# A decoder block with three token mixers: rotation halves copied by DMA, inputs loaded a step ahead, other orders of work

## The chip, the cores and the metric

One core of a Trainium2 chip runs the whole program. The metric is the device time of an execution in microseconds. A core has TensorE (PE: matmuls and transposes into PSUM), VectorE (DVE), ScalarE (ACT), GpSimd (POOL), and SyncE (SP), which here only issues DMAs. Each of them works through its own list of instructions in order and waits on semaphores.

## The reference

The input is x, 1024 rows of 1024 float32 values, with the weights of one layer:

```
h = RMSNorm(x);  P = h @ W_in                      # 1024 x 9248, split by columns
a = retention(rotary(rq), rotary(rk), rv)          # 4 heads of 128, chunks of 128
    rotary(x1|x2) = (x1*cos - x2*sin | x1*sin + x2*cos)
a = (silu(rg) * group_norm(a)) @ ret_w_o
b = group_norm(ssd(conv(sxbc), dt) * silu(sz)) @ ssd_w_o     # 16 heads of 64, 2 groups
c = (silu(gr) * group_norm(gla(gq, gk, gv, gate))) @ gla_w_o # 4 heads, keys 64, values 128
x = x + (sig(g_a)*a + sig(g_b)*b + sig(g_c)*c) @ W_out
x = x + relu(RMSNorm(x) @ W_up)^2 @ W_down
y = RMSNorm(x)
```

Retention, SSD and GLA are recurrences over eight chunks of 128 rows: a product inside the chunk, and a state carried on to the next.

## The kernel before

All arithmetic is at float32 accuracy, made from three matmuls in the faster format `fp32r`: every operand is split into a rounded part and its remainder (`split`, lines 155 to 157: ScalarE rounds, VectorE subtracts), and `acc3` (line 159) adds high x high, high x low and low x high in PSUM. Nearly all of TensorE's matmuls stand at line 164, and most weights pass through `wslot` (line 150): a DMA into one of two raw buffers, then a split into one of four pairs.

*Start.* `x_rows` (line 227) loads 128 rows and scales them by their norm, `x_chunk` transposes them on TensorE (line 244) and splits the result (`he` for even chunks, `ob` and `hb` for odd ones); `v_unit` (line 284) multiplies a chunk by the value weights.

*Projections.* `run_set` (line 340) computes 256 columns of P by seven products instead of eight (Strassen's scheme): seven steps of 12 matmuls each, with partial sums `us` on VectorE (line 358) that the next product into the same PSUM bank must wait for. `projections` (line 387) goes through the sets, prepares the next set's weights in between, and after each step runs one function of the list `later`. For four of the sets (rotary q and k of two head pairs) a result tile goes through `e_rot` (line 420): `turn` multiplies each half of 64 partitions by sin into the other half of `rb` (line 433), multiplies the tile by cos (line 434), adds both on GpSimd (line 435) and stores the tile to HBM (line 403).

*Mixers.* `merge` (line 915) interleaves generators: after each step of the main one as many steps of the mixer as its share says. `ret_mixer` (line 596) loads per chunk one tile `rin` of six blocks (q, k and gate of two heads, line 606) into one of three buffers, and `rv` into one of two. `stage_a` makes scores, `stage_b` outputs and the state, and `finish_heads` (line 575) normalizes, transposes (line 589) and multiplies by the gate, which is read from `rin`, one step later. `ssd_mixer` (line 670) runs beside 27 gate steps, and then `ssd_rows` (line 774) takes a power on GpSimd (line 177), transposes and stores it. `gla_mixer` (line 783) loads one tile `gin` of 14 blocks per chunk (line 800) and runs beside the first two branches of the output.

*Output.* For each half of the rows `branch_part` (line 1039) multiplies the heads of one branch (0 retention, 1 SSD, 2 GLA) by its weights, eight steps of 12 matmuls (24 for SSD), multiplies by the gate on VectorE (line 1054) and adds the branches on GpSimd (line 1058). In the last branch the sum is split into `mh` and `ml`, which `out_half` (line 1065) multiplies by W_out, 256 columns at a time; its first 63 matmuls use all but the last of the eight tiles. Normalization and the MLP follow.

The order of instructions on each engine is fixed when the program is built. A planner goes through time by its own estimates of durations and lets an engine take the first instruction, in the order of the program text, whose inputs and buffers are ready. A load can thus stand far ahead of its place in the text, as soon as its buffer is free; its place in the text decides only which of several ready ones goes first. At run time that order doesn't change.

Of the kernel before, what the change touches and what calls it, by code (L numbers as in the profile page):

```python
# [18 lines left out]
P = 128  # L19
# [32 lines left out]
def _layout(inp):  # L52
# [38 lines left out]
    a["c_cos"] = np.ascontiguousarray(np.concatenate([cos, cos]))  # L91
    a["c_sin"] = np.ascontiguousarray(np.concatenate([sin, -sin]))
    lg = np.log1p(-np.exp2(f(-5.0) - np.arange(RH, dtype=f))).astype(f)
# [18 lines left out]
def block_kernel(ctx, tc, i, out):  # L112
# [113 lines left out]

    def x_rows(c):
        xr = pro.tile([P, D], F32, name="xr")
        nc.sync.dma_start(out=xr, in_=i["x"][c])
        sq = pro.tile([P, D], F32, name="xsq", bufs=1)  # L230
        ss = wk.tile([P, 1], F32, name="ssx", tag="ss", bufs=6)
        S.activation(out=sq, in_=xr, func=AF.Square, accum_out=ss)
        v = wk.tile([P, 1], F32, name="vsx", tag="ss", bufs=6)
        V.tensor_scalar(out=v, in0=ss, scalar1=1.0 / D, scalar2=EPS, op0=ALU.mult, op1=ALU.add)
        r = wk.tile([P, 1], F32, name="rsx", tag="ss", bufs=6)
        G.tensor_tensor(out=r, in0=v, in1=nhalf[:, 0:1], op=ALU.pow)
        S.activation(out=xr, in_=xr, func=AF.Copy, scale=r)
        return xr
# [167 lines left out]
    def halves(t):  # L406
        return t.rearrange("p (j q t) -> q p j t", q=2, t=P)
# [12 lines left out]
    def e_rot(p, slot0):  # L420
        def emit(n, par, ps, other):
            r = ev.tile([P, 512], F32, name="ra", tag="w2k")
            if other is None:
                S.copy(out=r, in_=ps)
            else:
                V.tensor_tensor(out=r, in0=ps, in1=other, op=ALU.add)

            def turn():
                b = rp.tile([P, 512], F32, name="rb", tag="rb", bufs=2)
                r3, b3 = (t.rearrange("p (j t) -> p j t", t=P) for t in (r, b))  # L430
                for q in range(2):
                    src, to = slice(64 * q, 64 * q + 64), slice(64 - 64 * q, 128 - 64 * q)
                    V.tensor_tensor(out=b3[to], in0=r3[src], in1=halves(sin)[par][src], op=ALU.mult)
                V.tensor_tensor(out=r3, in0=r3, in1=halves(cos)[par], op=ALU.mult)
                G.tensor_tensor(out=r, in0=r, in1=b, op=ALU.add)
                put_T(rt_d[p], slot0 + n, par, r)
            later.append(turn)
        return emit
# [157 lines left out]
    def ret_mixer(p):  # L596
# [4 lines left out]
        for t, n, w in ((dm, "c_dm", 2 * P), (qd, "c_qd", 2 * P), (kd, "c_kd", 2)):  # L601
            nc.sync.dma_start(out=t, in_=i[n][:, p * w:(p + 1) * w])

        def stage_a(c):
            rin = rm.tile([P, 6, P], F32, name="rin", bufs=3)
            nc.sync.dma_start(out=rin, in_=rt_d[p][c])
            rv = rm.tile([P, 256], F32, name="rv")
            nc.sync.dma_start(out=rv, in_=rv_d[p][c])
            sc = pmx.tile([P, 512], F32, name="mx", tag="mx")
# [19 lines left out]
        def stage_b(c):  # L629
            rin, rv, sm, qs, ks = live.pop(c)  # L630
            state = st["s"]
            o = pmx.tile([P, 512], F32, name="mx", tag="mx")
# [5 lines left out]
            if c + 1 < NT:  # L638
# [12 lines left out]
                st["s"] = new  # L651
            return finish_heads(o[:, 0:256], rin[:, 4:6, :], o_d[p][c // 4][:, :, c % 4, :])

        pend = None
        stage_a(0)
        yield
# [117 lines left out]
    def ssd_rows():  # L774
        r = rstd(wk, ssq, SH // SG * SP, 2 * NT)
        pt = ptp.tile([P, 512], F32, name="tp", tag="tp")
        PE.transpose(out=pt[0:2 * NT, 0:P], in_=r, identity=ident)
        rt = wk.tile([2 * NT, P], F32, name="ysr", tag="whalf", bufs=2)
        V.tensor_copy(out=rt, in_=pt[0:2 * NT, 0:P])
        nc.sync.dma_start(out=ys_d, in_=rt)  # L780


    def gla_mixer():
# [11 lines left out]
        ins = {}  # L795

        def stage_a(c, q_):
            if q_ == 0:
                gin = gp.tile([P, 14, P], F32, name="gin", bufs=3)
                nc.sync.dma_start(out=gin, in_=gt_d[c])  # L800
                ins[c] = gin
            gin = ins[c]
# [129 lines left out]
    for _ in range(24):  # L932
        PE.matmul(out=wz[:, 0:128], lhsT=ones, rhs=ones, start=True, stop=True)
    xn = {0: x_rows(0)}
    w0 = [wslot(i["w_vdg"][q], 1152) for q in range(2)]
    xn[1] = x_rows(1)
    w1 = [wslot(i["w_v"][q]) for q in range(2)]
    hc = {0: x_chunk(0, xn[0])}
    xn[2] = x_rows(2)
    raws, cur = {}, {}  # L940
    for c in range(NT):
        if c + 1 < NT:
            hc[c + 1] = x_chunk(c + 1, xn.pop(c + 1))
            if c + 3 < NT:
                xn[c + 3] = x_rows(c + 3)
            if c % 2 == 0:
                x_comb(c // 2)
        v_unit(c, hc[c], 0, w0)
        if c < NT - 2:
            v_unit(c, hc[c], 1, w1)  # L950
        if c == 3:
            raws[0], raws[1] = fetch(jobs[0][1]), fetch(jobs[1][1])
# [34 lines left out]
    rm = rmst.enter_context(tc.tile_pool(name="rm", bufs=2))  # L987
    merge(run(4), 28, itertools.chain(ret_mixer(0), ret_mixer(1)), 38)
    rmst.close()
# [10 lines left out]
    sp = sst.enter_context(tc.tile_pool(name="sp", bufs=2))  # L1000
    merge(itertools.islice(main, 27), 27, itertools.chain(ssd_mixer(0), ssd_mixer(1)), 38)
    ssd_rows()
    sst.close()
# [32 lines left out]

    accs = {}

    def branch_part(h, b, o):
        first = (0, 4, 12)[b]  # L1040
        ws = None
        for d in range(KD):
            if b == 1 or d % 2 == 0:
                ws = wslot(i["w_o"][first + (d if b == 1 else d // 2)])
            pool, tag = (ev, "w2k") if b else (bp, "macc")
            gt = pool.tile([P, 512], F32, name="gt", tag=tag, bufs=8 if b == 0 else 4)
# [8 lines left out]
            if b == 0:  # L1055
                accs[d] = gt
            else:
                G.tensor_tensor(out=accs[d], in0=gt, in1=accs[d], op=ALU.add)
            if b == 2:
                m = (mp.tile([P, 512], F32R, name="mh"), mp.tile([P, 512], F32R, name="ml"))  # L1060
                split(m[0], m[1], accs[d])
                merged[d] = m
            yield

    def out_half(h):
# [4 lines left out]
        for s in range(4):  # L1070
            ws = [wslot(i["w_out"][s, q]) for q in range(2)]
            ps = [None] * 4
# [50 lines left out]
    mixer = gla_mixer()  # L1123
    merge(branch_part(0, 0, o), 8, zip_steps(itertools.islice(parts, 6), itertools.islice(mixer, 6)), 6)
    merge(branch_part(0, 1, o), 8, mixer, 12)
    for _ in parts:
# [6 lines left out]
    mp = mst.enter_context(tc.tile_pool(name="mp", bufs=8, side="right"))  # L1133
    for _ in branch_part(0, 2, o):
        pass
# [6 lines left out]
    merge(rest, 8, load_o(1, o, range(16)), 16)  # L1142
    for b in range(3):
        for _ in branch_part(1, b, o):
            pass
# [177 lines left out]
```

## Time and profile before

| | |
|---|---|
| Time, median of 3 runs | 1921.67 us (1919.79 to 1925.02) |
| Profiled execution, its own time | 1922.45 us |
| Its span | 1920.7 us |
| PE busy | 1870.8 us (97%) |
| DVE busy | 1134.4 us (59%) |
| ACT busy | 825.2 us (43%) |
| POOL busy | 216.3 us (11%) |
| Mean granted clock of PE | 0.993 |

The span runs from the first to the last instruction of the profiled execution. Busy times are shares of the whole span; TensorE's matmuls are pipelined and their ends modelled, so busy doesn't mean at its peak. A row `A <- B` in the list of waits says that A stood still until B was done. In the rows, `L164` is line 164 of the kernel, `SPq` a DMA issued by SP, and a tile's buffer number is left out.

### The profile page before, as it was taken

How to read it: one execution, taken by the hardware profiler on the slowest of the kernel's cores; microseconds unless marked ns; L12 is line 12 of the kernel's file. 1: busy time of each engine (PE TensorE's matmuls, PEld its weight loads, DVE VectorE, ACT ScalarE, POOL GpSimd, SP SyncE). 2: the span in 40 equal slices, each digit the busy share in tenths (PEclk: the TensorE clock that was granted, in tenths of full speed). 3: DMA queues.
4: the chain of work that ended last, by engine and by line, in shares of the span. 5: the costliest groups of instructions: out<-in, count | busy, mean ns of one | idle time of the engine just before them, and what ended most of it. 6: DMA issues, size and time to landing. Idle time of an engine off the chain costs nothing. (4 is left out here: it accounts for less than half of the span.)

```text
span 1920.7 us, 24987 instructions
## 1 busy us (share of the span) xinstructions
PE 1870.8 (97%) x9372; PEld 1542.8 (80%) x9372; DVE 1134.4 (59%) x1719; ACT 825.2 (43%) x1438; POOL 216.3 (11%) x223
## 2 busy tenths in 40 slices
PE   8999999999999999999999999999999999999998
PEld 8977778888777777777888988988888888888886
DVE  6877766667545476746776445585555444444444
ACT  7522333334445597855663113354444431211213
POOL 0011100000121043321232023000000000000003
PEclk9999999999999999999999999999999999999999
DMA  6423323333653666538467543642232362332222
GB/s 215 144 88 98 114 88 119 110 107 92 196 152 116 224 203 192 174 101 284 148 206 257 187 127 121 222 164 103 101 119 93 120 246 89 97 101 88 89 73 92
DMA packets 169465, 271.69 MB, mean 141 GB/s; under 512 B 11616, under 2 KB 110976, under 8 KB 162688
## 3 DMA queue, kind: packets, MB, share of 16 engines
q1 hardware_dynamic: 168768, 269.18, 43.3%
q8 instruction: 74, 1.21, 0.2%
q10 hardware_dynamic: 576, 0.92, 0.1%
q14 instruction: 47, 0.39, 0.1%
HBM read 191.33 MB, written 78.72 MB: 141 GB/s over the span
## 5 line engine op out<-in xcount | busy, mean ns | idle before, releaser
L156 ACT CAST whi<-raw 128x1024 fp32r<-128x1024 f32 (+1 forms) x223 | 233.6, 1050 | 515.4 <-PE mm L164 464.1
L157 DVE TENSOR_TENSOR wlo<-raw,whi 128x1024 fp32r<-128x1024 f32 (+1 forms) x223 | 281.1, 1261 | 127.0 <-ACT whi L156 125.6
L164 PE MATMUL mm<-ht,whi 128*128 128x512 f32 x936 | 296.8, 398 | 6.8 <-DVE us L358 6.8
L164 PEld LDWEIGHTS mm<-ht,whi 128*128 128x128 f32 x936 | 175.5, 188 | 52.1 <-DVE us L358 8.6
L164 PE MATMUL mm<-he,whi 128*128 128x512 f32 x672 | 214.7, 399 | 1.2 <-ACT us L364 0.9
L164 PE MATMUL mm<-whi,ah 128*128 128x512 f32 x512 | 202.5, 395 | 0.0
L164 PE MATMUL mm<-wlo,ah 128*128 128x512 f32 x512 | 202.5, 395 | 0.0
L164 PE MATMUL mm<-whi,al 128*128 128x512 f32 x512 | 202.5, 395 | 0.0
L164 PE MATMUL mm<-ht,wlo 128*128 128x512 f32 x468 | 185.6, 397 | 0.0
L1267 DVE TENSOR_TENSOR x<-mm,x 128x512 f32<-128x512 f32 x128 | 88.2, 689 | 158.8 <-PE mm L164 158.8
L164 PEld LDWEIGHTS mm<-he,whi 128*128 128x128 f32 x672 | 125.2, 188 | 32.4 <-issue 1.7
L164 PE MATMUL mm<-hb,whi 128*128 128x512 f32 x464 | 149.0, 401 | 0.7 <-DMA hb<-b 0.7
L164 PE MATMUL mm<-he,wlo 128*128 128x512 f32 x336 | 133.7, 398 | 0.0
L164 PE MATMUL mm<-ht,w 128*128 128x512 f32 x468 | 116.3, 396 | 0.0
L164 PEld LDWEIGHTS mm<-wlo,ah 128*128 128x128 f32 x512 | 96.2, 188 | 23.4
L164 PEld LDWEIGHTS mm<-whi,ah 128*128 128x128 f32 x512 | 96.2, 188 | 23.2
L164 PEld LDWEIGHTS mm<-whi,al 128*128 128x128 f32 x512 | 96.2, 188 | 23.2
L358 DVE TENSOR_TENSOR us<-mm,us 128x512 f32<-128x512 f32 x78 | 53.8, 690 | 89.1 <-PE mm L164 87.7
L164 PEld LDWEIGHTS mm<-ht,wlo 128*128 128x128 f32 x468 | 88.1, 188 | 21.5
L164 PEld LDWEIGHTS mm<-ht,w 128*128 128x128 f32 x468 | 87.7, 188 | 21.0
L164 PEld LDWEIGHTS mm<-hb,whi 128*128 128x128 f32 x464 | 86.2, 188 | 22.2 <-issue 1.7
L164 PE MATMUL mm<-ohi,whi 128*128 128x512 f32 x256 | 103.9, 406 | 0.0
(281 smaller groups left out, 3544.3 us busy)
## 6 DMA issues: line engine op xcount, KB each, us to landing
raw<-w_in SPq DMA_DIRECT2D x34, 1024.0 KB, 5.4
raw<-w_o SPq DMA_DIRECT2D x32, 512.0 KB, 4.1
raw<-w_up SPq DMA_DIRECT2D x16, 1024.0 KB, 4.9
act<-rl SPq DMA_DIRECT2D x64, 256.0 KB, 2.0
raw<-w_down SPq DMA_DIRECT2D x32, 512.0 KB, 4.3
araw<-act SPq DMA_DIRECT2D x64, 256.0 KB, 3.4
gate<-gt SPq DMA_DIRECT2D x48, 256.0 KB, 2.9
gt<-gate SPq DMA_DIRECT2D x48, 256.0 KB, 4.8
```

The source lines that it names most:

```text
L156: S.copy(out=dst_hi, in_=src)
L157: V.tensor_tensor(out=dst_lo, in0=src, in1=dst_hi.bitcast(F32), op=ALU.subtract)
L164: PE.matmul(out=ps, lhsT=l, rhs=r, start=(first and j == 0), stop=(last and j == n - 1), skip_group_check=open_)
L358: V.tensor_tensor(out=t, in0=ps, in1=other, op=ALU.add)
L1267: V.tensor_tensor(out=xs, in0=ps, in1=xs, op=ALU.add)
```

## The change

Seven edits in one:

- Rotation: two DMAs copy the halves of a result tile crosswise into a tile `rb` as soon as it is made, and `turn` multiplies the tile by cos into a new tile and the copy by sin in place, both over 128 partitions, with the sign now in the constant.
- Retention: q and k blocks and values are loaded by `load_in`, called for chunk c + 1 in `stage_a(c)`; the gate blocks have a tile `rg` of their own, loaded in `stage_b`.
- Start: x rows and first weights are loaded by DMAs that stand first in the text; the first value product stands ahead of the second chunk's work.
- SSD: the mixer runs beside 26 steps, and `ssd_rows` is a generator around the 27th.
- GLA: the first `gin` is loaded, and its memory cleared, ahead of the first branch; the mixer's first step comes after four branch steps instead of two.
- Output: in the last branch the sums of tiles 6 and 7 are on VectorE, and the first W_out weights are fetched at tile 6.
- Second half: branches run in the order 0, 2, 1, so that SSD (24 matmuls per step) is last.

```diff
     a["c_cos"] = np.ascontiguousarray(np.concatenate([cos, cos]))
-    a["c_sin"] = np.ascontiguousarray(np.concatenate([sin, -sin]))
+    a["c_sin"] = np.ascontiguousarray(np.concatenate([-sin, sin]))
     lg = np.log1p(-np.exp2(f(-5.0) - np.arange(RH, dtype=f))).astype(f)
...
-    def x_rows(c):
+    def x_load(c):
         xr = pro.tile([P, D], F32, name="xr")
         nc.sync.dma_start(out=xr, in_=i["x"][c])
+        return xr
...
+    def x_rows(xr):
         sq = pro.tile([P, D], F32, name="xsq", bufs=1)
...
+            b = rp.tile([P, 512], F32, name="rb", tag="rb", bufs=3)
+            for q in range(2):
+                nc.sync.dma_start(out=b[64 - 64 * q:128 - 64 * q], in_=r[64 * q:64 * q + 64])
...
             def turn():
-                b = rp.tile([P, 512], F32, name="rb", tag="rb", bufs=2)
                 r3, b3 = (t.rearrange("p (j t) -> p j t", t=P) for t in (r, b))
-                for q in range(2):
-                    src, to = slice(64 * q, 64 * q + 64), slice(64 - 64 * q, 128 - 64 * q)
-                    V.tensor_tensor(out=b3[to], in0=r3[src], in1=halves(sin)[par][src], op=ALU.mult)
-                V.tensor_tensor(out=r3, in0=r3, in1=halves(cos)[par], op=ALU.mult)
-                G.tensor_tensor(out=r, in0=r, in1=b, op=ALU.add)
-                put_T(rt_d[p], slot0 + n, par, r)
+                a = rp.tile([P, 512], F32, name="rc", tag="rc", bufs=2)
+                a3 = a.rearrange("p (j t) -> p j t", t=P)
+                V.tensor_tensor(out=a3, in0=r3, in1=halves(cos)[par], op=ALU.mult)
+                V.tensor_tensor(out=b3, in0=b3, in1=halves(sin)[par], op=ALU.mult)
+                G.tensor_tensor(out=a, in0=a, in1=b, op=ALU.add)
+                put_T(rt_d[p], slot0 + n, par, a)
             later.append(turn)
...
+        ins = {}
...
+        def load_in(c):
+            rin = rm.tile([P, 4, P], F32, name="rin", bufs=3)
+            nc.sync.dma_start(out=rin, in_=rt_d[p][c][:, 0:4])
+            rv = rm.tile([P, 256], F32, name="rv", bufs=3)
+            nc.sync.dma_start(out=rv, in_=rv_d[p][c])
+            ins[c] = rin, rv
...
         def stage_a(c):
-            rin = rm.tile([P, 6, P], F32, name="rin", bufs=3)
-            nc.sync.dma_start(out=rin, in_=rt_d[p][c])
-            rv = rm.tile([P, 256], F32, name="rv")
-            nc.sync.dma_start(out=rv, in_=rv_d[p][c])
+            if c + 1 < NT:
+                load_in(c + 1)
+            rin, rv = ins.pop(c)
             sc = pmx.tile([P, 512], F32, name="mx", tag="mx")
...
             rin, rv, sm, qs, ks = live.pop(c)
+            rg = rm.tile([P, 2, P], F32, name="rg")
+            nc.sync.dma_start(out=rg, in_=rt_d[p][c][:, 4:6])
             state = st["s"]
...
                 st["s"] = new
-            return finish_heads(o[:, 0:256], rin[:, 4:6, :], o_d[p][c // 4][:, :, c % 4, :])
+            return finish_heads(o[:, 0:256], rg, o_d[p][c // 4][:, :, c % 4, :])
...
         pend = None
+        load_in(0)
+        yield
         stage_a(0)
...
         r = rstd(wk, ssq, SH // SG * SP, 2 * NT)
+        yield
         pt = ptp.tile([P, 512], F32, name="tp", tag="tp")
...
         nc.sync.dma_start(out=ys_d, in_=rt)
+        yield
...
+        def load_in(c):
+            ins[c] = gp.tile([P, 14, P], F32, name="gin", bufs=3)
+            nc.sync.dma_start(out=ins[c], in_=gt_d[c])
...
+        load_in(0)
+        yield
...
         def stage_a(c, q_):
-            if q_ == 0:
-                gin = gp.tile([P, 14, P], F32, name="gin", bufs=3)
-                nc.sync.dma_start(out=gin, in_=gt_d[c])
-                ins[c] = gin
+            if q_ == 0 and c + 1 < NT:
+                load_in(c + 1)
             gin = ins[c]
...
         PE.matmul(out=wz[:, 0:128], lhsT=ones, rhs=ones, start=True, stop=True)
-    xn = {0: x_rows(0)}
-    w0 = [wslot(i["w_vdg"][q], 1152) for q in range(2)]
-    xn[1] = x_rows(1)
+    def v_raw(name, q, n):
+        raw = wp.tile([P, n], F32, name="raw", tag="raw", bufs=2)
+        nc.sync.dma_start(out=raw, in_=i[name][q])
+        return raw
...
+    rows_in = {0: x_load(0)}
+    raw0 = [v_raw("w_vdg", q, 1152) for q in range(2)]
+    rows_in[1] = x_load(1)
+    xn = {0: x_rows(rows_in.pop(0))}
+    w0 = [wparts(None, raw, 1152) for raw in raw0]
+    hc = {0: x_chunk(0, xn.pop(0))}
+    xn[1] = x_rows(rows_in.pop(1))
     w1 = [wslot(i["w_v"][q]) for q in range(2)]
-    hc = {0: x_chunk(0, xn[0])}
-    xn[2] = x_rows(2)
+    rows_in[2] = x_load(2)
     raws, cur = {}, {}
     for c in range(NT):
+        if c == 0:
+            v_unit(c, hc[c], 0, w0)
         if c + 1 < NT:
             hc[c + 1] = x_chunk(c + 1, xn.pop(c + 1))
+            if c + 2 < NT:
+                xn[c + 2] = x_rows(rows_in.pop(c + 2))
             if c + 3 < NT:
-                xn[c + 3] = x_rows(c + 3)
+                rows_in[c + 3] = x_load(c + 3)
             if c % 2 == 0:
                 x_comb(c // 2)
-        v_unit(c, hc[c], 0, w0)
+        if c > 0:
+            v_unit(c, hc[c], 0, w0)
         if c < NT - 2:
...
     rm = rmst.enter_context(tc.tile_pool(name="rm", bufs=2))
-    merge(run(4), 28, itertools.chain(ret_mixer(0), ret_mixer(1)), 38)
+    merge(run(4), 28, itertools.chain(ret_mixer(0), ret_mixer(1)), 40)
     rmst.close()
...
     sp = sst.enter_context(tc.tile_pool(name="sp", bufs=2))
-    merge(itertools.islice(main, 27), 27, itertools.chain(ssd_mixer(0), ssd_mixer(1)), 38)
-    ssd_rows()
+    merge(itertools.islice(main, 26), 26, itertools.chain(ssd_mixer(0), ssd_mixer(1)), 38)
+    tail = ssd_rows()
+    next(tail)
+    merge(itertools.islice(main, 1), 1, tail, 1)
     sst.close()
...
-    def branch_part(h, b, o):
+    first_out = []
...
+    def branch_part(h, b, o, last=False):
         first = (0, 4, 12)[b]
...
                 ws = wslot(i["w_o"][first + (d if b == 1 else d // 2)])
+            if last and d == 6:
+                first_out.extend(wslot(i["w_out"][0, q]) for q in range(2))
             pool, tag = (ev, "w2k") if b else (bp, "macc")
...
             else:
-                G.tensor_tensor(out=accs[d], in0=gt, in1=accs[d], op=ALU.add)
-            if b == 2:
+                (V if last and d > 5 else G).tensor_tensor(out=accs[d], in0=gt, in1=accs[d], op=ALU.add)
+            if last:
                 m = (mp.tile([P, 512], F32R, name="mh"), mp.tile([P, 512], F32R, name="ml"))
...
         for s in range(4):
-            ws = [wslot(i["w_out"][s, q]) for q in range(2)]
+            ws = [first_out.pop(0) if s == 0 else wslot(i["w_out"][s, q]) for q in range(2)]
             ps = [None] * 4
...
     mixer = gla_mixer()
-    merge(branch_part(0, 0, o), 8, zip_steps(itertools.islice(parts, 6), itertools.islice(mixer, 6)), 6)
-    merge(branch_part(0, 1, o), 8, mixer, 12)
+    next(mixer)
+    main = branch_part(0, 0, o)
+    merge(itertools.islice(main, 2), 2, itertools.islice(parts, 2), 2)
+    merge(main, 6, zip_steps(itertools.islice(parts, 4), itertools.islice(mixer, 5)), 5)
+    merge(branch_part(0, 1, o), 8, mixer, 13)
     for _ in parts:
...
     mp = mst.enter_context(tc.tile_pool(name="mp", bufs=8, side="right"))
-    for _ in branch_part(0, 2, o):
+    for _ in branch_part(0, 2, o, True):
         pass
...
     merge(rest, 8, load_o(1, o, range(16)), 16)
-    for b in range(3):
-        for _ in branch_part(1, b, o):
+    for b in (0, 2, 1):
+        for _ in branch_part(1, b, o, b == 1):
             pass
```

## Rows read from the trace of the kernel before

**Rows 1.** The page's busy line of TensorE: us, share of the span, instructions.

```profile
PE 1870.8 (97%) x9372; PEld 1542.8 (80%) x9372; DVE 1134.4 (59%) x1719; ACT 825.2 (43%) x1438; POOL 216.3 (11%) x223
```

**Rows 2.** Waits of TensorE: total us, number of waits, longest.

```profile
PE mm L164 <- DVE us L358: 6.8, 4, 1.8
PE mm L164 <- ACT mh L156: 5.4, 3, 2.3
PE mx L611 <- DMA rin<-rt: 4.9, 7, 1.7
PE tp L244 <- ACT xr L237: 4.1, 2, 2.2
PE tp L805 <- DMA gin<-gt_d: 4.0, 1, 4.0
PE tp L589 <- ACT og L583: 3.3, 6, 0.9
PE tp L854 <- ACT gv L807: 2.8, 3, 1.4
PE tp L777 <- POOL rs_r L177: 2.6, 1, 2.6
```

**Rows 3.** Windows: length, busy us per engine, granted clock (PEclk), DMA share, GB/s.

```profile
15.00:21.50 6.50, 6.09 (x25) 5.80 (x26) 6.46 (x11) 6.14 (x10) 1.48 (x2) 0.52 0.85 260
245.20:250.20 5.00, 5.00 (x15) 3.96 (x16) 2.33 (x3) 1.96 (x3) 0.00 (x0) 0.66 0.29 82
896.70:902.00 5.30, 5.22 (x15) 4.17 (x16) 3.21 (x13) 3.56 (x10) 0.46 (x1) 0.51 0.99 385
1038.40:1042.00 3.60, 3.60 (x20) 3.60 (x19) 1.34 (x2) 2.24 (x3) 1.30 (x1) 0.53 0.22 81
1178.50:1182.00 3.50, 3.45 (x15) 3.23 (x16) 2.42 (x3) 0.95 (x1) 2.03 (x1) 0.53 0.07 6
250.00:490.00 240.00, 240.00 (x1031) 192.89 (x1030) 166.12 (x205) 93.31 (x109) 0.00 (x0) 1.00 0.35 107
1186.00:1250.00 64.00, 64.00 (x550) 64.00 (x550) 38.20 (x61) 25.81 (x34) 3.86 (x7) 1.00 0.58 202
```

**Rows 4.** Timelines of the start: start, length, instruction, idle time before it.

```profile
11.38 0.68 DVE L246 TENSOR_TENSOR xe<-tp,k_cols 128x512 f32<-128x512 f32 x1
14.12 1.04 ACT L156 CAST he<-xe 128x1024 fp32r<-128x1024 f32 x1
15.22 0.61 PE L164 MATMUL mm<-whi,he 128*128 128x288 f32 x1 [0.79 <-ACT he L156]
```

**Rows 5.** Window of one set of rotated tiles; the other three are alike.

```profile
101.80:121.20 19.40, 17.80 (x77) 14.01 (x76) 19.02 (x25) 4.02 (x5) 6.40 (x4) 1.00 0.32 101
```

**Rows 6.** Groups by line from 100 to 250 us: busy us, mean ns.

```profile
L433 DVE TENSOR_TENSOR rb<-ra,k_c_sin 64x512 f32<-64x512 f32 x32 | 25.7, 804 | 0.9
L434 DVE TENSOR_TENSOR ra<-ra,k_c_cos 128x512 f32<-128x512 f32 x16 | 11.0, 686 | 0.1
```

**Rows 7.** DMA issues from 100 to 250 us: KB each, median us to landing.

```profile
rt<-ra SPq DMA_DIRECT2D x16, 256.0 KB, 2.4
```

**Rows 8.** Timeline of SP's queue in the retention mixer.

```profile
500.77 0.52 SPq L592 DMA_DIRECT2D o<-ot  x1
501.34 0.60 SPq L606 DMA_DIRECT2D rin<-rt  x1
```

**Rows 9.** Timelines of GpSimd and SP before the first GLA input.

```profile
886.83 0.31 POOL L793 MEMSET qbd<- 128x256 f32 x1 [27.70 <-PE mm L164]
889.06 0.42 SPq L800 DMA_DIRECT2D gin<-gt_d  x1
```

**Rows 10.** Timelines of VectorE, GpSimd and ScalarE in the last branch, first half.

```profile
1034.21 0.68 DVE L1054 TENSOR_TENSOR gt<-mm,gt 128x512 f32<-128x512 f32 x1
1035.04 1.26 POOL L1058 TENSOR_TENSOR gt<-gt 128x512 f32<-128x512 f32 x1 [2.12 <-DVE gt L1054]
1036.33 0.62 ACT L156 CAST mh<-gt 128x512 fp32r<-128x512 f32 x1 [2.77 <-POOL gt L1058]
```

## The prediction

> **What bounds the kernel now.** First the page's busy line: TensorE is busy 1870.8 of 1920.7 us [rows 1], so it sets the time, and a change pays only where it shortens a stretch in which TensorE stands still or runs slow. Second the waits of TensorE alone [rows 2]: the eight rows shown are 33.9 us, and their causes differ. 6.8 us go to VectorE's partial sums of line 358, in four waits of up to 1.8; 5.4 to the rounding of the merged tile `mh`, three waits; 4.9 to the retention input `rin`, seven; 4.1 to the first x rows; 4.0 to the first GLA input `gin`, one wait; 2.6 to the SSD statistic `rs_r`, one. Third the windows with the granted clock [rows 3]. After some of these waits TensorE runs at the lower of its levels (1.2 instead of 2.4 GHz) for some us. The loss is length times (1 - clock): 6.5 x 0.48 = 3.1 us at the start, 5.0 x 0.34 = 1.7 behind the last wait on line 358, 5.3 x 0.49 = 2.6 behind `gin`, 3.6 x 0.47 = 1.7 and 3.5 x 0.47 = 1.6 behind the two groups of waits for `mh`. So a removed wait can be worth more than its row in the list. Two prices for later: 240 us hold 1031 matmuls of 512 columns [rows 3], 0.233 us each, so a step of 12 is 2.8 us and one of 24 is 5.6; of 256 columns 64 us hold 550, 0.116 each.
>
> **The start.** TensorE's first projection matmul comes at 15.22, released by ScalarE's rounding of `he`, which started at 14.12, though VectorE had its input done at 12.06 (11.38 + 0.68) [rows 4]; ScalarE did work of the second x block and of later weights in between. The change puts that work behind the first product. The rounding can then start 2 us sooner, but the 1.09 us of transposes that TensorE did before 15.22 follow later instead. I take 1.0 us for that and 0.5 for the clock coming back sooner: -1.5. Bounds: 0 (another order, same chain) and -6 (the longer wait for `xr`, 2.2 [rows 2], the 0.79 before 15.22, and the 3.1 of clock).
>
> **The rotation.** A tile costs VectorE two products of 64 partitions, 804 ns each, and one of 128, 686 ns [rows 6]: 2.29 us. After, it is two of 128 partitions: 1.37. That is 0.92 less, and 3.7 for the four tiles of one set. In such a set VectorE is busy 19.0 of 19.4 us while TensorE needs 17.8 [rows 5]: here VectorE is the bound, and what is behind is the wait of line 358. With 3.7 less it needs 15.3, which is 2.5 below TensorE, so all four waits (6.8) and the clock loss behind the last (1.7) can go: -8.5. Added are two copies per tile, 32 on SP's queue, and a wait: the product with `sin` needs the copy to have landed. Everything behind it on VectorE (sums of line 358, weight remainders) stands while it waits. SP's queue also holds the stores of finished tiles, which wait for GpSimd, so that a copy behind one is late. The trace has no copy between SBUF tiles; the nearest row is the 256 KB store of this stage, 2.4 us to landing [rows 7]. If VectorE finds other work for that time, the hold w is 0; if it finds none, 2.4 per tile. Its need is 15.3 + 4w, so waits come back from w = 0.6, and at w = 1.0 it is back at 19.3 and nothing is won. I take w between 0.3 and 0.7, because the instructions are put in order with the landing in mind and VectorE has the next weights' work to place there, and the late copies eat part of it: -6.5. Bounds -8.5 and +26.7 (w = 2.4, priced below).
>
> On these two copies a rule of the Trainium skill speaks against the change (DMA: Bandwidth & Descriptors, section Rules for kernel authors): transfers to two disjoint partition halves are served one after the other, and one transfer over 128 partitions should be used. No row here shows two half transfers; the 2.4 us above are of a full one. With that page's fixed 2 us and half the ports for each half, an estimate is 3.2 us to the second landing, 0.8 later than the row; all of it in w would leave waits of 0.7 per set and a gain of some 4 instead of 6.8 in waits.
>
> **Retention inputs.** SP issues the load of `rin` at 501.34, directly behind a finished head's store at 500.77 [rows 8]: the buffer is held by the gate half of the tile until the head is finished, and the load starts with hardly a lead over its use. The change does more than move the load: it takes the gate out of `rin` (two of six blocks, loaded for itself), so the buffer is free once the scores are made. The load then leads by a chunk, far over what it takes, and is a third smaller. Cost: eight more issues per mixer on SP, 0.6 each, beside a queue that has gaps. 4.9 us of waits [rows 2]: -4.5. Bounds -4.9 and +1.
>
> **SSD statistic.** One wait of 2.6; now a step of 24 matmuls (5.6 us) lies between the GpSimd power and the transpose that needs it, and the mixer is packed into 26 steps instead of 27. -2.5, bounds -2.6 and 0.
>
> **First GLA input.** GpSimd starts to clear this stage's memory at 886.83, when TensorE lets the region go; the load is issued at 889.06, behind a weight and a mask [rows 9], and TensorE waits 4.0 us for it [rows 2]. The change issues it ahead of the branch's weights (some 1.5 us sooner) and puts the first GLA step behind four output steps instead of two, 5.6 us later. Sooner plus later is 7 us against a wait of 4.0: it goes, with its clock loss of 2.6. Against it, 13 mixer steps instead of 12 fall on the next eight steps. -6.2, bounds -6.6 and +2.
>
> **Last sums of a stage.** In the last branch one step is a chain: VectorE product at 1034.21, GpSimd sum at 1035.04 for 1.26, ScalarE rounding at 1036.33 for 0.62 [rows 10], and VectorE's remainder, about 0.7 like its product; the next product comes only behind it, 3.4 us after the last, against TensorE's 2.8. The lag grows over eight steps. *First half:* only the sums of steps 6 and 7 move to VectorE, 0.68 instead of 1.26 and a hand-over; the lag of steps 0 to 5 stays. The wait shrinks by 0.8 of 2.3, and the clock loss of 1.7 goes with a chance of a quarter: -1.2, bounds -4.0 and +1. *Second half:* the SSD branch is now last, whose steps take 5.6 us; the chain of 3.4 fits, no lag builds up, and the last tile's chain (about 2.7) lies under the 63 matmuls x 0.116 = 7.3 us that don't need it. What is left of `mh`, 5.4 - 2.3 = 3.1 us, and the clock loss of 1.6 go: -4.7, bounds -4.7 and 0.
>
> **What is late next.** TensorE now comes sooner to the finished heads (`og`, 3.3 us) and to GLA's transposes (2.8 behind `gv`) [rows 2]; a third more of each is +2, bounds 0 and +6. First weights of the output product loaded ahead: 0, no row shows a wait for them.
>
> **Sum.** -1.5 - 6.5 - 4.5 - 2.5 - 6.2 - 1.2 - 4.7 + 2.0 = -25.1. The profiled execution took 1922.45 us (span 1920.7 and 1.75 around it), 0.8 above the median of 1921.67; 1922.45 - 25.1 = 1897.
>
> **Rivals.** *The copy eats the rotation's gain* (w about 1.0): the rotation gives 0, the sum is -18.6, 1904. For it: the waiting product holds a VectorE queue that had 0.4 us free in a set. Against: 3.7 us of work leave that queue. *Slower, by the copy:* w at the full 2.4. VectorE needs 15.3 + 9.6 = 24.9 per set, TensorE waits 7.1, four sets 28.4 instead of 6.8, and three more stretches at the low clock at 1.7: +26.7; with the other terms, -18.6, 1930.5. From w = 1.9 on nothing is won in all, from 2.3 on it is slower by over 0.3%. For it, the four tiles of a set come 2.8 to 5.6 us apart, with GpSimd's stores in the same SP queue. Against: there is other ready work on VectorE in the same set. *Ahead in name only:* a load starts when its buffer is free, wherever it stands in the program; if retention and GLA inputs don't come sooner, 10.7 us are missing, 1908, and together with the first rival 1914.5. For it: the load right behind the store [rows 8]. Against: the gate's own tile frees that buffer.
>
> **How the numbers follow.** Forecast 0.64 (own range 1888 to 1902), copy eats the gain 0.18, in name only 0.12, slower 0.06. Range 1887 to 1911: below, all lower bounds together without new waits would be -37 (1885), and 1887 stands for most of them; above, the third case with half of the first. A run can tell 0.3% (5.8 us) from no change: faster, under 1915.9, is 0.64 + 0.18 + half of the third case = 0.88; no change 0.06 (the other half, where it meets the first); slower 0.06.
>
> **What would show it.** The waits of TensorE: line 358 under 2 us (else w is over 0.6), no `rin`, `gin` or `rs_r` row; `mh` left once, under 2 us, in the first half only; no stretch at the lower clock behind the first GLA input and in the second half's output product. In the rotation, VectorE under 17 us in a set, and its wait for the copied tile under 0.7 per tile. Wrong it would be if VectorE's `sin` product waits 1 us or more, if a new row over 4 us stands in that list, or if TensorE's busy time grows as its waits fall.

## The result, and the profile after

The changed kernel takes 1895.28 us (median, 1892.40 to 1895.74) against 1921.57 for the kernel before, a ratio of 0.9858 (95% interval 0.9841 to 0.9875). The forecast was 1897.0. Its profiled execution took 1895.59 us, span 1893.8, so the two profiled executions differ by 26.9 us; all that follows splits this number.

TensorE's busy line of the page after (it answers to [rows 1]) shows 7 us less busy time and nearly 20 us less idle time:

```profile
PE 1863.7 (98%) x9372; PEld 1540.5 (81%) x9372; DVE 1129.8 (60%) x1707; ACT 817.6 (43%) x1432; POOL 204.6 (11%) x219
```

TensorE's waits after (total us, number, longest; they answer to [rows 2]). `gin` and `rs_r` are gone and `rin` nearly (0.3), `mh` is left once, the sums (now line 361) fell from 6.8 to 2.2; a new row, `kk`, heads the list:

```profile
PE tp L886 <- ACT kk L881: 4.2, 2, 3.3
PE mm L164 <- ACT he L156: 2.3, 2, 2.0
PE mm L164 <- DVE us L361: 2.2, 4, 0.6
PE tp L247 <- ACT xr L240: 2.2, 3, 1.7
PE tp L879 <- ACT gv L832: 2.0, 3, 1.0
PE tp L595 <- ACT og L589: 1.4, 2, 1.0
PE mm L164 <- ACT mh L156: 1.0, 1, 1.0
PE mx L658 <- ACT og L589: 0.9, 1, 0.9
```

Windows after with the granted clock (columns as in [rows 3] and [rows 5]): the first three are its stretches at the lower level, at the start, behind `kk`, and behind the norm of the first half (one more, of 1.6 us, stands at the very end, as in the kernel before); the fourth is one set of rotated tiles. The stretches behind the sums and in both output products are gone; the third is new, and the last row, of the kernel before, shows that stage there at full clock:

```profile
12.00:18.70 6.70, 5.29 (x22) 4.95 (x23) 3.96 (x6) 5.23 (x6) 1.03 (x2) 0.53 0.62 192
888.70:892.10 3.40, 3.40 (x11) 2.87 (x11) 2.78 (x10) 3.28 (x14) 0.00 (x0) 0.50 0.19 72
1226.60:1233.50 6.90, 6.14 (x29) 6.14 (x30) 6.90 (x9) 3.69 (x5) 0.00 (x0) 0.51 0.64 249
101.30:120.70 19.40, 18.85 (x82) 14.85 (x80) 17.44 (x22) 4.86 (x6) 5.86 (x4) 1.00 0.52 149
```

```profile
1250.00:1265.00 15.00, 12.73 (x104) 11.87 (x103) 14.42 (x19) 9.42 (x13) 0.00 (x0) 1.00 0.51 175
```

Where the time went, by the starts of the same TensorE instructions in the two timelines (us; the stage is the distance of two marks):

| stage, from mark to mark | before | after | difference | forecast |
|---|---|---|---|---|
| start, to the last product of the first projection's `he` | 68.77 | 68.20 | -0.6 | -1.5 |
| rotation and later projections, to the first `rin` product | 423.46 | 417.08 | -6.4 | -6.5 |
| retention, to the first `xin` product | 167.62 | 158.77 | -8.9 | -4.5 |
| SSD, to the first branch product | 226.76 | 224.46 | -2.3 | -2.5 |
| GLA, to the first output product | 145.29 | 144.19 | -1.1 | -6.2 |
| output halves, to the first norm transpose | 160.43 | 150.97 | -9.5 | -5.9 |
| norm and the rest | 730.12 | 731.92 | +1.8 | part of +2.0 |

The sum was right to 1.8 us because errors of both signs cancelled: retention and output brought 8 us more than forecast, GLA 5 less. That much of it is luck. Two matmuls (0.5 us) that stand ahead of the first `rin` product before, in e1 and in e3 stand behind it after and in the other runs, so that the rotation's difference is rather -5.9 and retention's -9.3.

Each kernel has one profiled execution, and the stretches at the lower clock differ between executions of one kernel: the mean granted clock of the four executions of the kernel after runs from 0.994 to 0.996, and 0.002 of the span is some 4 us. A stage's difference of 1.7 us, the price of a stretch of 3.4 us at half the clock, is therefore not safe as the effect of an edit.

### The profile page after: what moved, and what is told of

It is laid out like the page before. It is cut to its first block, busy times and chain, and to the rows that moved or that the text cites. A ratio compares the mean times of both kernels' runs of the same rounds, so it can differ in the third digit from the quotient of the medians.

```text
span 1893.8 us, 25031 instructions
## 1 busy us (share of the span) xinstructions
PE 1863.7 (98%) x9372; PEld 1540.5 (81%) x9372; DVE 1129.8 (60%) x1707; ACT 817.6 (43%) x1432; POOL 204.6 (11%) x219
## 5 line engine op out<-in xcount | busy, mean ns | idle before, releaser
L157 DVE TENSOR_TENSOR wlo<-raw,whi 128x1024 fp32r<-128x1024 f32 (+1 forms) x223 | 288.1, 1293 | 138.7 <-ACT whi L156 131.7
```

Of the source, the lines that this page charges most:

```text
L157: V.tensor_tensor(out=dst_lo, in0=src, in1=dst_hi.bitcast(F32), op=ALU.subtract)
```

## The experiments

Times are medians of several runs beside runs of the kernel before, to which the ratios go (the kernel after: 0.9858); a "stage" is a row of the table above, read from the one profiled execution of a kernel.

**e1: the rotation alone.** The kernel before with this edit (and the sign of `c_sin` that goes with it):

```diff
+for q in range(2):
+    nc.sync.dma_start(out=b[64 - 64 * q:128 - 64 * q], in_=r[64 * q:64 * q + 64])
...
-    V.tensor_tensor(out=b3[to], in0=r3[src], in1=halves(sin)[par][src], op=ALU.mult)
+V.tensor_tensor(out=b3, in0=b3, in1=halves(sin)[par], op=ALU.mult)
```

> The kernel before with the rotation's edit alone (two half copies by DMA, products on 128 partitions), all else as before. Theory: the copies land under other work of VectorE, so the edit alone gives what the two traces show between the first projection and the first retention matmul, 6.4 us; the first retention matmul comes near 492.2 - 6.4 = 485.8 us, and the time is 1913.5 to 1917, as later stages keep their waits. Rival 1 (the copy eats the gain): first retention matmul within 1 us of 492.2, time 1920 to 1923. Rival 2 (the gain of that stretch is owed to the new start, which shifts what VectorE has to do beside the rotation): 2 to 4 us, 1918 to 1920.

Measured: 1915.82 us, ratio 0.9965 (0.9952 to 0.9978). The rotation's stage fell by 6.2 us (423.46 to 417.30), the profiled execution as a whole by 6.1. The theory holds; the start's edit has no part in it.

**e2: twice the copy.**

```diff
-    nc.sync.dma_start(out=b[64 - 64 * q:128 - 64 * q], in_=r[64 * q:64 * q + 64])
+nc.sync.dma_start(out=sw, in_=r)          # sw in DRAM
+    nc.sync.dma_start(out=b[64 - 64 * q:128 - 64 * q], in_=sw[64 * q:64 * q + 64])
```

> The kernel after, but each half rotation goes through DRAM: the tile is stored (256 KB) and its two halves are read back swapped, so that the copied tile lands two transfers after the tile is made, about 5 us instead of 2.6. All is computed as before. Theory: VectorE has other work to place while a tile lands, so the hold w stays under 0.6 per tile and the first retention matmul comes at most 3 us later than 485.3 (time up to 1898). Rival (the 2.6 us only just fit, VectorE's order leaves no more): each tile holds VectorE some 2.4 us more, which in the prediction's pricing is about 25 us for the four sets, 1917 to 1923, with new waits of TensorE on the partial sums of line 361 of 4 us and more a set.

Measured: 1889.55 us, ratio 0.9825 (0.9811 to 0.9840): not slower but faster, which neither theory had. The stage took 413.55 us, 3.5 less than after, and the waits on line 361 were gone. VectorE did wait for the longer copies (2.7 us in all), but TensorE waited for none of it. So the copy's length doesn't matter, and something else held VectorE in the kernel after. Its timeline beside GpSimd's shows it (start, length, instruction):

```profile
105.64 1.21 DVE L439 TENSOR_TENSOR rc<-ra,k_c_cos 128x512 f32<-128x512 f32 x1
112.88 1.78 DVE L329 TENSOR_TENSOR raw<-raw 128x512 f32<-128x512 f32 x1
115.90 1.67 DVE L334 TENSOR_TENSOR raw<-raw 128x512 f32<-128x512 f32 x1
118.70 0.68 DVE L361 TENSOR_TENSOR us<-mm,us 128x512 f32<-128x512 f32 x1
```

```profile
105.01 1.29 POOL L441 TENSOR_TENSOR rc<-rc,rb 128x512 f32<-128x512 f32 x1 [52.02 <-PE mm L164]
112.44 1.66 POOL L441 TENSOR_TENSOR rc<-rc,rb 128x512 f32<-128x512 f32 x1 [6.14 <-DVE rb L440]
115.40 1.62 POOL L441 TENSOR_TENSOR rc<-rc,rb 128x512 f32<-128x512 f32 x1 [1.29 <-DVE rb L440]
118.85 1.28 POOL L441 TENSOR_TENSOR rc<-rc,rb 128x512 f32<-128x512 f32 x1 [1.83 <-DVE rc L439]
```

GpSimd's sums end at 106.30, 114.10 and 117.02; the VectorE operations that started meanwhile end at 106.85, 114.66 and 117.57, each 0.55 later, as if their work of 0.68 had begun only when the sum was nearly over. The sum of line 361, which reads PSUM, started 0.15 before the fourth of GpSimd's, and both kept their usual lengths (0.68 and 1.28). In e2 fewer VectorE operations start during one of GpSimd's sums: lines 329 and 334 take 0.68 and 0.69 there.

**e12: GpSimd's sum taken away.**

```diff
-G.tensor_tensor(out=a, in0=a, in1=b, op=ALU.add)
+V.tensor_tensor(out=a, in0=a, in1=b, op=ALU.add)
```

> The kernel after with the rotation's last sum (rc + rb) on VectorE instead of GpSimd, which is then idle in that stage. In the kernel after, VectorE operations of 512 columns that start while GpSimd's sum runs take 1.2 to 1.8 us instead of 0.68, each ending some 0.55 us after the sum. Theory (GpSimd's sum holds VectorE's operations on SBUF operands up): they all fall back to 0.68 to 0.69 us; VectorE gains about 2.8 us per set and has four sums of 0.68 more, so that its busy time in a set (18.0 in 20 us) stays within 0.3; the waits on line 361 and the time stay within 2 us of the kernel after. Rival (the long operations come from the copies' DMA traffic or from what the products read): they stay, VectorE is at 20 us and more in a set, the waits on line 361 grow to 4 us and more, time 1898 to 1905.

Measured: 1889.68 us, ratio 0.9831 (0.9814 to 0.9849). Groups by line from 100 to 240 us (busy us, mean ns), after and then e12:

```profile
L439 DVE TENSOR_TENSOR rc<-ra,k_c_cos 128x512 f32<-128x512 f32 x16 | 12.6, 786 | 0.3
L329 DVE TENSOR_TENSOR raw<-raw 128x512 f32<-128x512 f32 x7 | 9.2, 1309 | 0.0
L334 DVE TENSOR_TENSOR raw<-raw 128x512 f32<-128x512 f32 x7 | 8.8, 1251 | 0.2
```

```profile
L439 DVE TENSOR_TENSOR rc<-ra,k_c_cos 128x512 f32<-128x512 f32 x16 | 11.0, 687 | 0.4 <-DMA rt<-rc 0.2
L441 DVE TENSOR_TENSOR rc<-rc,rb 128x512 f32<-128x512 f32 x16 | 11.0, 686 | 0.1
L334 DVE TENSOR_TENSOR raw<-raw 128x512 f32<-128x512 f32 x7 | 4.8, 688 | 0.1
L329 DVE TENSOR_TENSOR raw<-raw 128x512 f32<-128x512 f32 x7 | 4.8, 685 | 0.0
```

All long operations are back at 0.69 us, though the copies run as before; the rival is out. The Trainium skill (SBUF — State Buffer, section SBUF: two separate sides) says that VectorE and GpSimd share a pair of ports under a lock which the one that starts first keeps for its whole instruction, and that a VectorE operation takes part in this if both inputs lie in SBUF; these rows agree. A row of the kernel before agrees on the other side: a sum with a PSUM input (line 426) that started 0.9 us into a GpSimd sum took its usual 0.68:

```profile
104.86 2.15 POOL L435 TENSOR_TENSOR ra<-ra,rb 128x512 f32<-128x512 f32 x1 [53.04 <-DVE ra L434]
105.77 0.68 DVE L426 TENSOR_TENSOR ra<-mm,us 128x512 f32<-128x512 f32 x1
```

The theory's second half was too careful, and the time fell by 5.6 us where it was to stay within 2: the waits on line 361 didn't stay, they went. In the first set one of the four moved sums and one weight operation now stand behind that line's sum. That set in the same 20 us, after, e2 and e12 (columns as in [rows 5]):

```profile
101.00:121.00 20.00, 19.45 (x84) 15.35 (x83) 18.04 (x22) 4.86 (x6) 5.86 (x4) 1.00 0.50 144
```

```profile
101.00:121.00 20.00, 20.00 (x87) 16.06 (x87) 15.71 (x22) 5.04 (x7) 4.55 (x4) 1.00 0.57 187
```

```profile
101.00:121.00 20.00, 20.00 (x87) 16.09 (x86) 17.38 (x25) 4.88 (x7) 0.00 (x0) 1.00 0.56 162
```

In both variants TensorE has no gap left and the stage takes the same time, 413.5 us.

**e3 and e4: the two halves of the retention edit, undone one at a time.**

```diff
# e3
-rin = rm.tile([P, 4, P], F32, name="rin", bufs=3)
+rin = rm.tile([P, 6, P], F32, name="rin", bufs=3)   # gate in it again
# e4
-    if c + 1 < NT:
-        load_in(c + 1)
+    load_in(c)
```

> The kernel after with the gate put back into the retention's input tile (one load of six blocks, as before), still issued a step ahead. Theory (the gate's own tile is what pays: with it in, the buffer is held until a head is finished): the waits for rin come back, 4 to 8 us; the retention stage (ScalarE's first SSD work minus the first retention matmul, 125.5 us after, 134.1 before) takes 130 to 134 us, time 1899 to 1904. Rival (issuing a step ahead is what pays; three buffers are enough with or without the gate): the stage stays under 127 us and the time within 1894 to 1897.

> The kernel after with the gate's own tile kept, but the retention inputs issued in the step that uses them, as before. Theory (the gate's own tile pays, the step ahead in the program does not, because a load starts when its buffer is free): the stage stays within 2 us of 125.5, time 1894 to 1898. Rival (the step ahead pays): the waits for rin come back, the stage takes 130 to 134 us, time 1899 to 1904. If both this kernel and the one with the gate put back lose 4 us or more, the two edits only pay together.

Measured: e3 1902.61 us, ratio 0.9891 (0.9875 to 0.9908), the expectation's stage 132.2 us; e4 1895.27, 0.9856 (0.9842 to 0.9871), 125.8. TensorE's waits in this stage, e3 and then e4:

```profile
PE mx L625 <- DMA rin<-rt: 3.5, 6, 1.0
PE tp L595 <- ACT og L589: 2.5, 4, 0.8
```

```profile
PE mx L624 <- DMA rin<-rt: 0.6, 2, 0.3
PE tp L595 <- ACT og L589: 0.4, 1, 0.4
PE mx L657 <- ACT og L589: 0.3, 1, 0.3
```

The theories of both hold, though `rin` came back with 3.5 us and not the 4 to 8 expected. The gate's own tile is 6.6 of the 8.9 us (table's marks: 165.40 in e3; 7.1 with the two matmuls named under the table counted alike). In e1, whose retention is the old one, the stage takes 166.31: so issuing a step ahead is worth 0.9 at most while the gate holds the buffer, and nothing once it doesn't (158.69 in e4). The load came no sooner for standing earlier in the program.

**e5, e6 and e14: the first GLA step.** e5 undoes that part; e6 gives the first `gin` a buffer that is free earlier; e14 moves one copy.

```diff
# e6
+gin0 = bp.tile([P, 14, P], F32, name="gin0", bufs=1)
+nc.sync.dma_start(out=gin0, in_=gt_d[0])            # before the branches
...
-    load_in(0)
+    ins[0] = gin0
# e14
-    S.copy(out=kk, in_=tk[:, 0:P])
+    V.tensor_copy(out=kk, in_=tk[:, 0:P])
```

> The kernel after with the GLA part undone (the first inputs loaded inside their step, behind the branch's first weights, and the first step back between the second and third output step). Theory, from the two traces: the edit only exchanged one wait for another, so undoing it costs at most 1.5 us between the first branch product and the first output product (144.2 us after, 145.3 before): the wait for gin comes back at 3 to 5 us, the one for kk (3.3) goes; time 1894 to 1898. Rival (the edit is worth what the prediction gave it, 6.2 us, and something else lost it): that stretch takes 148 us or more, time 1900 and above.

> The kernel after with the first GLA input in a buffer of its own in a pool that is free when the branches start, so that its load is issued before the stage's memory is let go; the rest as after. Theory (the landing of this tile, 7.8 us after issue, is the shared cause of the old wait for gin and of the new one for kk): both waits go, 3 to 4 us, with the stretch at the low clock behind them, 1.7; from the first branch product to the first output product 139 to 141 us instead of 144.2, time 1890 to 1892. Rival (ScalarE's work, a table load and some 20 exponentials placed ahead of the copy of kk, sets it, whenever the input lands): the wait for kk stays at 2 us or more and the stretch at 143 to 145 us.

> The kernel after with the copy of kk (128x128 out of PSUM) on VectorE instead of ScalarE. Theory (the copy only waits because it stands behind exponentials in ScalarE's queue: its input was there at 884.8, it started at 888.13): the wait for kk falls under 1 us, the stretch from the first branch product to the first output product from 144.2 to 140 to 142 us, time 1891 to 1893. Rival (what is late is the whole first step, since its input landed late): the next product that needs this step (the one with scm) waits in its place, 2 us or more, and the stretch stays over 143 us.

Measured: e5 1896.78 us, 0.9868 (0.9853 to 0.9883), stage 144.25 against 144.19; e6 1891.40, 0.9842 (0.9827 to 0.9857), 142.69; e14 1891.92, 0.9845 (0.9830 to 0.9860), 138.84. So the edit as made is worth nothing in its stage: it changed a wait for `gin` (3.3 in e5) into one for `kk`. The timelines after show why. GpSimd's first clearing at 868.74 marks the moment at which the memory is let go, and the load is issued 2.3 us later, behind a weight and a mask, just as in [rows 9]; the input lands and ScalarE starts at 878.94 with a table load; the copy of `kk` comes at 888.13, behind the exponentials of later steps:

```profile
868.74 0.31 POOL L813 MEMSET qbd<- 128x256 f32 x1 [30.48 <-PE mm L164]
871.02 0.42 SPq L819 DMA_DIRECT2D gin<-gt_d  x1
878.94 1.28 ACT L847 ACT_TABLE_LOAD   x1 [1.47 <-DMA gin<-gt_d]
888.13 0.25 ACT L881 COPY kk<-tp 128x128 f32<-128x128 f32 x1
888.43 0.97 PE L886 MATMUL tp<-gv,kk 128*128 128x256 f32 x2 [3.25 <-ACT kk L881]
```

With the input early (e6) the first step's exponentials are done at 877, yet TensorE waits as long (2.2 before the transpose of `kt` and 0.9 for `kk`), since ScalarE still does the second block's exponentials ahead of the copies that the first step needs. What e6 gains here, 1.5 us, is the low-clock stretch behind, absent in it: the idle time of the stage is the same (8.05). With the copy on VectorE (e14) the scores' mask takes the place of the first wait, 2.6, but the later small waits shrink and the low clock is gone too: -5.4 in this stage, -3.4 in the whole time. The difference lies in part in the output, where e14 takes 153.39 us against 150.97: its wait for `mh` is 1.6 instead of 1.0, with 3.4 us at the lower clock behind it. Both theories of e6 and e14 hold in part: one late thing hides the next.

**e8 and e7: last sums.** e8 puts the second half's branches back into the order 0, 1, 2; e7 the first half's last two sums back on GpSimd.

```diff
# e8
-for b in (0, 2, 1):
-    for _ in branch_part(1, b, o, b == 1):
+for b in range(3):
+    for _ in branch_part(1, b, o, b == 2):
# e7
-(V if last and d > 5 else G).tensor_tensor(out=accs[d], in0=gt, in1=accs[d], op=ALU.add)
+(V if last and d > 5 and h == 1 else G).tensor_tensor(out=accs[d], in0=gt, in1=accs[d], op=ALU.add)
```

> The kernel after with the second half's branches in the old order (the last one is again the one with steps of 12 products, 2.8 us each), its last two sums on VectorE. Theory (the order is what pays in the second half: a step of 2.8 us is shorter than its chain of about 3.4, one of 5.6 is not): the waits for mh come back in the second half, about 1 to 2.5 us, with a stretch at the low clock of 1.6; time 1897 to 1900. Rival (the last two sums on VectorE alone do it): no new wait for mh over 0.5 us, time 1894 to 1896.

> The kernel after with the first half's last two sums on GpSimd again (the second half as after). Theory (the first half is worth the 2.5 us which the waits for mh fell by there, and the stretch at the low clock behind them comes back at most in part): from the first output product to the first transpose of the norm 152.5 to 155 us instead of 150.97, time 1897 to 1899. Rival, the prediction's price: 0.8 in waits and at most 0.4 of clock, 151.8 to 152.2, time 1896 to 1897.

Measured: e8 1899.73 us, 0.9883 (0.9866 to 0.9899), stage 156.49 against 150.97; e7 1895.40, 0.9859 (0.9841 to 0.9877), stage 153.17. Waits for `mh`, e8 and then e7:

```profile
PE mm L164 <- ACT mh L156: 3.4, 3, 1.6
```

```profile
PE mm L164 <- ACT mh L156: 1.6, 1, 1.6
```

The order is worth 5.5 us: 2.4 of waits for `mh`, 0.2 for `ml`, 1.7 of clock, the rest not in rows; e8's theory holds. e7's stage is 2.2 longer: 0.6 of wait, near the 0.8 that the prediction priced, and a low-clock stretch of 3.4 us (1.7). But this is not shown to be the price of VectorE's sums alone: e5 and e14 keep them on VectorE, and there the first half's wait for `mh` is 1.6 too, with the same stretch behind it, and the stage takes 153.63 and 153.39. In these profiles the first half's waits of 1.6 to 2.3 (before, e1, e5, e7, e14) all have the stretch behind them, and those of 1.0 (the kernel after and six others) have none. e7's time missed both its theory and its rival; its norm is 1.2 us shorter, with 3.4 us at the lower clock where the kernel after has 6.9, and its start 0.4.

**x_best and x_best2: together.** The half rotation through DRAM (e2), `kk` on VectorE (e14) and all of a stage's last sums on VectorE; x_best2 with e6's early input too.

```diff
-(V if last and d > 5 else G).tensor_tensor(out=accs[d], in0=gt, in1=accs[d], op=ALU.add)
+(V if last else G).tensor_tensor(out=accs[d], in0=gt, in1=accs[d], op=ALU.add)
```

> What the runs so far point to, on the kernel after: the half rotation through DRAM (3 us of waits and later gaps), the copy of kk on VectorE (3 to 5 us), and all of a stage's last sums on VectorE, in both halves (up to 1.2 us, the last wait for mh). Theory (they are in three different stages and add up): 1884 to 1887 us. Rival (the second and third put VectorE over TensorE's step in the branches, so that waits for gt or scm come in their place): 1888 to 1891.

> The same with the first GLA input loaded early into a buffer of its own. Theory (with the copy of kk off ScalarE, what is left in the first step, 2.6 us before the product with scm, hangs on that input's landing): 1 to 3 us less than without it, 1882 to 1885. Rival (it hangs on the next block's input, whose work stands ahead in the fixed order): the same as without it within 1 us.

Measured: x_best 1885.59 us, ratio 0.9809 (0.9792 to 0.9826); x_best2 1882.69, 0.9792 (0.9774 to 0.9809), the fastest. Both theories hold. In x_best2 no row of `kk`, `scm`, `mh` or line 361 is left; with the copy off ScalarE's queue the early input does pay (GLA stage 139.84 to 138.01). Its first rows, the start ahead of all:

```profile
PE mm L164 <- ACT he L156: 2.5, 2, 2.0
PE tp L247 <- ACT xr L240: 2.1, 3, 1.6
PE tp L881 <- ACT gv L834: 1.6, 3, 1.1
```

e12's way of the rotation's sum was not tried in this set.

## Why the prediction was right, point by point

- **Start, -1.5: measured -0.6.** The first product came 2.0 us sooner (15.22 to 13.20), but the waits for `he` and `xr` only fell from 4.9 to 4.5 us in all, and as much ran at the lower clock (6.8 us). Not run by itself; the twelve profiles with this start have 67.6 to 68.8 us, the two with the old one 68.8 and 69.9: on average 1.1 less, with a spread as large.
- **Rotation, -6.5: measured -6.4, e1 -6.2.** The sum was right, its reason was not, so that its closeness is luck. The prediction took 3.7 us per set off VectorE and explained what would be left by the hold w of the copy. VectorE never waited for a copy in the kernel after, so w was 0; yet it was busy 17.4 us in a set, where under 17 was forecast. GpSimd's sums hold it up, and they did so in the kernel before already. Two of its groups from 100 to 250 us show it, beside line 433 of [rows 6], which takes 0.69 us alone and up to 1.27 beside a sum:

```profile
L157 DVE TENSOR_TENSOR w<-raw,w 128x512 fp32r<-128x512 f32 x7 | 7.8, 1116 | 0.0
L327 DVE TENSOR_TENSOR raw<-raw 128x512 f32<-128x512 f32 x7 | 7.7, 1102 | 1.4 <-PE mm L164 1.2
```

- **Rotation, what the prediction's 3.7 us was.** Beyond 0.69 us for each operation these two groups have 3.0 and 2.9 us and line 433 has 3.6: 9.5 us of hold in the four sets. After, the three groups shown under e12 have 9.9, some 2.5 per set. So the 804 ns of [rows 6] was a mixture; the edit freed 0.69 us per tile and 2.8 per set, not 0.92 and 3.7, and the hold moved on to other operations. The term w = 0.3 to 0.7 was a real loss of the right size put down to the wrong cause; its sign in the list of what would show it, "under 2 us (else w is over 0.6)", came out at 2.2 and would have misled.
- **The rule on two half transfers.** Each half of 128 KB landed 2.6 us (median) after its own issue, and the issues are 0.52 apart (median), so the second is there 3.2 us after the first issue, the estimate's number. Whether the two halves are served in turn or are only issued in turn, these rows can't tell. What hung on it, a longer hold, did not come: e2 doubles the way and loses nothing.
- **Retention, -4.5: measured -8.9, the term most under-sized.** The mechanism is right (e3). In the stage TensorE's idle time fell from 9.8 to 3.3 us, `rin` by 4.6 and `og` by 1.1 where growth was priced; its busy time fell by 2.4, so that a removed wait was worth more than its row; why it fell stays open. 1.3 of the 8.9 came with the rotation alone (e1).
- **SSD, -2.5: measured -2.3.** By the traces alone; `rs_r` has no row.
- **GLA, -6.2: measured -1.1, the step that failed.** Of "sooner plus later" the later half came: TensorE reaches the first input 11.8 us after the first branch product instead of 10.2 behind a wait of 4.0, and finds it landed. "Some 1.5 us sooner" did not: it was read off the code's order, but the buffer's release and the two transfers still ahead set the issue, 2.5 us after the first branch product before and after. What lost the gain is the next step of the argument, "it goes, with its clock loss": it took the wait for the input for all that was late in this step. ScalarE's exponentials and copies behind the landing were late too, and `kk` cost 3.3 us in its place, with a stretch of 3.4 us at the lower clock behind it; the stage's idle time went from 8.5 to 8.1 only. The rival "ahead in name only" is true here; in retention its rule held too (e4), but there the gate's own tile freed the buffer.
- **Last sums, -1.2 and -4.7: measured -2.2 (e7) and -5.5 (e8).** The second half's mechanism is right. In the first half the stretch at the lower clock went, to which a chance of a quarter was given; but e5 and e14 have it back with the same sums, so what decides there stays open. Some 1.7 us of this stage's -9.5 belong to no run.
- **What is late next, +2.0.** `og` and `gv` shrank; what came late was `kk`; and the norm took 1.8 us more, with a stretch of 6.9 us at the lower clock (3.4) that it did not have before. A new row over 4 us, named as a sign of error, does stand in the list, and it marks the failed step.

## What to carry to other kernels

When work is taken off VectorE, look at what GpSimd runs beside it: two-input operations on SBUF stretched each other here, and it was the one that started second that was hit; a mean over such operations mixes lengths. A sum of 0.69 us on the busy engine was cheaper than 1.3 on the idle one. To get a load earlier, free its buffer (the gate's own tile) rather than move the line; and behind a removed wait follow the same step's later instructions in their engine's queue, since the next one may be late for the same reason. A removed wait was worth more than its row in the rotation (e2, e12) and in retention, and next to nothing in GLA. Take a stage's difference of 1.7 or 3.4 us with care where the clock may account for it.

## What the runs showed of the hardware that was not expected

- A VectorE operation of 0.68 us on SBUF operands took 1.2 to 1.8 us when it started during a GpSimd sum, ending 0.55 us after it; with GpSimd idle all were at 0.69. GpSimd's sum, 1.29 alone, took 1.62 to 1.66 when it started some 0.2 us after such a VectorE operation.
- Taking away four waits of 0.55 us on line 361 shortened that stage by 3.5 us (e2, e12), 0.9 each.
- The same three waits behind the norm (1.0, 0.4, 0.9 us before; 0.8, 0.4, 0.9 after) were followed by full clock before and in e14, by 6.9 us at the lower level in the kernel after, and by 3.4 in e6, e7, e12 and x_best2. One wait of 2.6 for `rs_r` was followed by full clock before and by 3.4 us at the lower level in e1.
